# A decode kernel's page stage: probability transposes, the next unit's rotary scores and the products with keys in one piece

## The chip, the cores and the metric

The kernel runs on one core of one Trainium2 chip. The time is device time in microseconds for one execution. TensorE (PE) runs matmuls and transposes in the order of its program, and so do VectorE (DVE), ScalarE (ACT) and GpSimd (POOL); SyncE (SP) issues most transfers, POOL the indirect ones. An engine waits for another through semaphores only. Every instruction's place in its engine's queue is fixed when the program is built.

## The reference: what is computed

One layer of a decoder with two mixers, retention and latent attention (MLA), for a prompt of 1,024 tokens and for 8 sequences that decode 4 tokens each. All inputs and results are float32. The change lies wholly in the latent attention of the 8 decoding sequences over their past, 8,192 tokens each, which lie in pages of 128 tokens. For a sequence with query rows of 8 heads x 4 tokens, a past token has a latent row `ckv` of 256 numbers and a rotary row `kr` of 64:

```
score = (q_latent . ckv + q_rotary . kr) * scale
out   = softmax(score over past and new tokens) . ckv
```

The queries are turned into the latent space beforehand, so that the latent row is key and value in one. New tokens are masked causally; past tokens are all seen.

## The kernel before

The kernel is a row of stages. In the page stage, some 550 us long, two streams of work are woven together. One is `page_attention`, the decoding sequences' attention. The other is `fill`, a generator of gate projections for the prompt: for each block of weights (`wh`, `wl`, the upper and lower part of a weight block, made by ACT L247 and DVE L199 from `wr`), each product of a 128x128 block with 352 columns takes three matmuls, L266, L267 and L268, into the bank `mm`; after eight blocks ACT writes the sum out (`gev`, L413). `fill` depends on nothing in the page stage, so it is what PE does while the attention waits for other engines.

`beside` weaves: `page_attention` is a Python generator that yields a number wherever projections may stand, and for each unit of that number `fill` gets its share, 321 of 505 in all, at 0.441 a step of three matmuls (a yield of 12.0 is some 52 matmuls). What stands between two yields is a piece. Then the framework's scheduler puts the instructions of each engine in an order of its own that mostly keeps this one, but can move an instruction past others that it does not depend on, and so lets projections into a piece or takes DVE's work ahead of its place.

Sequences are taken in four groups `g` of two, and a group's past in four parts `jj` of 16 pages a sequence: 16 units. Ahead of a group's first unit stands `new_tokens(g)`, which scores the new tokens (L607, L608), exponentiates them (`pn`: DVE L612 and L613, ACT L614), transposes the result on PE (L617, copied by DVE L619) and multiplies with the new latents (L622). A unit in `past_keys` is:

- Gather: POOL fetches rotary rows into `rr` and latent rows into `craw` by indirect transfers (L588, L589). `rr` has two buffers, `craw` four: a unit uses two of each.
- Scores, five steps (L642): first the rotary rows (j=8), then four times 64 of the latent's 256 numbers. In each, DVE transposes 32x32 blocks into one of two ring buffers `kt` (L648, four instructions), and PE multiplies with the queries `q4` (L652, 16 matmuls on 32x32 tiles) into `sc`, of which there is one. `q4` holds the queries of two groups; those of the other two are stored to `q4D` (L578) from the tile `sel`, which takes one of the two `kt` ring buffers, and are read back at g=2 (L715).
- Softmax: ACT copies half of `sc` (L663), DVE adds the other half and takes the minimum (L664), ACT exponentiates to `pr` (L668) and makes the correction of the earlier sums (L670).
- A yield of 12.0, then eight transposes of `pr` on PE in two fours (L677), each copied to `pT` by DVE or ACT (L678), with a yield of 1.0 behind each four.
- Products with the keys: 32 matmuls (L683), added to `acc` by DVE (L685), and a yield of 1.0.

`ended` closes a group (L690 on).

Of the kernel before, what the change touches and what calls it, by code (L numbers as in the profile page):

```python
# [9 lines left out]
F32 = mybir.dt.float32  # L10
# [151 lines left out]
def decode_step(ctx: ExitStack, tc: tile.TileContext, A: dict, O: dict):  # L162
# [316 lines left out]
    def big(name, shape, rows_=P):  # L479
        return p3.tile([rows_, *shape], F32, tag="craw", name=name, bufs=4)  # L480
# [4 lines left out]
    def ring(name):  # L485
        return p3.tile([P, 4, 512], F32, tag="kt", name=name, bufs=2)
# [94 lines left out]
    rows_c = A["cache_ckv"].rearrange("l n (s a) c -> (l n s) (a c)", a=NA)  # L581
    rows_r = A["cache_krope"].rearrange("l n (s a) c -> (l n s) (a c)", a=NA)

    def gather(b, jj, c, r):

        at_ = b * (NPG // NA) + jj
        off = bass.IndirectOffsetOnAxis(ap=idx[:, at_:at_ + 1], axis=0)
        pool.indirect_dma_start(out=r, out_offset=None, in_=rows_r, in_offset=off)  # L588
        pool.indirect_dma_start(out=c, out_offset=None, in_=rows_c, in_offset=off)  # L589

    def new_tokens(g):

# [31 lines left out]
        yield 1.0  # L624
        return st

    def past_keys(g, jj, st):

        rr = [p3.tile([P, NA * ROPE], F32, tag="rr", name="rraw", bufs=2) for _ in range(2)]
        cr = [big("craw", (NA * KL,)) for _ in range(2)]
        for s in range(2):
            gather(2 * g + s, jj, cr[s], rr[s])
        keys = [c.rearrange("p (a d) -> p a d", a=NA) for c in cr]
        rope = [r.rearrange("p (a d) -> p a d", a=NA) for r in rr]
        yield 5.0  # L640
        sc = psg.tile([P, 4, 512], F32, tag="sc", name="sc", bufs=1)
        steps = [8, *range(0, 8, 2)]  # L642
        for n, j in enumerate(steps):
            kt = ring("kt")
            for i in range(2):
                for s in range(2):
                    src = keys[s][:, :, 32 * (j + i):32 * (j + i) + 32] if j < 8 else rope[s][:, :, 32 * i:32 * i + 32]
                    dve.transpose(kt[:, 2 * i + s].rearrange("p (n r) -> p n r", r=32), src)  # L648
            for q in range(4):
                qs_ = slice(32 * q, 32 * q + 32)  # L650
                for v in range(4):
                    pe.matmul(sc[32 * v:32 * v + 32, q, :], Q["q4"][qs_, j + v // 2, 2 * (g % 2) + v % 2, :], kt[qs_, v, :], start=n == 0,  # L652
                              stop=n == NJ // 2 - 1, tile_position=(32 * q, 32 * v), skip_group_check=True)
            if n + 1 < len(steps):
                yield 2.5
        sums = mid("sums", (4, 8, 32))
        acc, l, nm = st["acc"], st["l"], st["nm"]
        nm2 = p3.tile([P, 1], F32, tag="nm", name="nm", bufs=4)
        for half in range(2):
            hs = slice(64 * half, 64 * half + 64)  # L660
            even, odd = (sc[o:o + 64, :, 256 * half:256 * half + 256] for o in (0, 64))
            out = sums[hs].rearrange("p q n x -> p q (n x)")
            act.copy(out, odd)  # L663
            dve.tensor_tensor_reduce(out=out, in0=even, in1=out, scale=-1.0, scalar=nm[hs], op0=ALU.add, op1=ALU.min, accum_out=nm2[hs])  # L664
        st["nm"] = nm2
        pr = mid("pr", (8, 4, 32))
        lb = p3.tile([P, 1], F32, tag="lb", name="lb", bufs=2)
        act.activation(pr.rearrange("p n q x -> p q n x"), sums, AF.Exp, scale=-1.0, bias=nm2, accum_out=lb)  # L668
        corr = p3.tile([P, 1], F32, tag="corr", name="corr", bufs=2)
        act.activation(corr, nm, AF.Exp, scale=-1.0, bias=nm2)  # L670
        dve.scalar_tensor_tensor(out=l, in0=l, scalar=corr, in1=lb, op0=ALU.mult, op1=ALU.add)
        yield 12.0
        pT = mid("pT", (8, P))
        for u in range(2):
            pt = xb()
            for a in range(4):
                pe.transpose(pt[:, a * P:(a + 1) * P], pr[:, 4 * u + a].rearrange("p q x -> p (q x)"), ident)  # L677
            (act.copy if u % 2 else dve.tensor_copy)(pT[:, 4 * u:4 * u + 4, :], pt.rearrange("p (a r) -> p a r", a=4))  # L678
            yield 1.0
        pv = xb()  # L680
        for n in range(8):
            for v in range(4):
                pe.matmul(pv[32 * v:32 * v + 32, :KL], pT[:, n, 32 * v:32 * v + 32], keys[v % 2][:, 8 * (v // 2) + n, :], start=n == 0,  # L683
                          stop=n == 7, tile_position=(0, 32 * v), skip_group_check=True)
        dve.scalar_tensor_tensor(out=acc, in0=acc, scalar=corr, in1=pv[:, :KL], op0=ALU.mult, op1=ALU.add)  # L685
        yield 1.0

    def ended(g, st):

# [19 lines left out]
        return acc  # L709

    def page_attention():
        for g in range(4):
            if g == 2:
                q4 = q4_tile()
                sp.dma_start(q4, q4D)  # L715
                Q["q4"] = q4
            st = yield from new_tokens(g)
            for jj in range(NPG // NA):
                yield from past_keys(g, jj, st)
            last = ended(g, st)  # L720
        spare = ring("out")
        outs = [spare[:, g, :KL] for g in range(3)]
        for g in range(3):
# [879 lines left out]
```

## Time and profile before

| | |
|---|---|
| median of three runs | 2174.16 us (2173.42 to 2175.05) |
| the profiled execution | 2180.01 us, span 2178.2 us |
| mean granted clock of PE | 0.998 |
| busy: PE / its weight loads | 2135.6 us (98%) / 1856.0 us (85%) |
| busy: DVE / ACT / POOL | 1237.5 us (57%) / 729.6 us (33%) / 324.5 us (15%) |
| projections L266, L267, L268 (`xh`, `xl`), 1344 each | 457.1, 435.4 and 434.4 us busy |
| score steps L652, 2560 records | 91.4 us busy |
| transposes into `kt`, L648 on DVE, 256 | 160.7 us busy |

A profile row gives start, duration, engine, line, operation, output <- inputs, and behind it in brackets the idle time ahead of it and what ended it. Rows of the same kind that follow each other are joined (x4), and a float32 matmul of the attention leaves two records, so that 16 score matmuls read as x32. PE's matmuls are pipelined: the distance between two starts says more than a duration.

### The profile page before, as it was taken

The page shows a single profiled execution, that of the slowest core. Times are in us where ns is not written, and L with a number is a line of the kernel's source. Part 1 is how long each engine was busy: PE and PEld are TensorE (multiplying, and loading weights), DVE is VectorE, ACT ScalarE, POOL GpSimd, SP SyncE. Part 2 cuts the span into 40 slices and gives each one's busy share as a digit, 9 for nine tenths or more (in the row PEclk, how much of TensorE's full clock was granted, in tenths as well). Part 3 has the DMA queues.
Part 4 walks back from the last instruction along what each step waited for, and adds up shares of the span by engine and source line. Part 5 has one row for each costly group of instructions (what it writes and reads, how often), then busy time and mean ns, then how long its engine had stood idle before and what let it go on. Part 6 is the DMA issues. An engine that isn't in the chain of part 4 may idle for free.

```text
span 2178.2 us, 38580 instructions
## 1 busy us (share of the span) xinstructions
PE 2135.6 (98%) x15368; PEld 1856.0 (85%) x15368; DVE 1237.5 (57%) x2788; ACT 729.6 (33%) x1537; POOL 324.5 (15%) x519
## 2 busy tenths in 40 slices
PE   8999999999999999999999999899999999999998
PEld 7998777777777898888788887788888999999998
DVE  5414564555645356657666664778677353444465
ACT  6412232333333232221222311454556342222243
POOL 2211111111110022222121220122121000000022
PEclk9999999999999999999999999999999999999999
DMA  8447566565665421533614517110111453234243
GB/s 238 139 134 270 203 229 220 188 248 206 222 219 185 124 67 49 172 116 88 205 45 122 181 49 247 61 36 12 38 51 56 148 198 98 80 98 124 78 140 118
DMA packets 264357, 299.72 MB, mean 138 GB/s; under 512 B 26544, under 2 KB 221744, under 8 KB 260080
## 3 DMA queue, kind: packets, MB, share of 16 engines
q1 hardware_dynamic: 254960, 213.36, 31.6%
q0 software_dynamic: 9216, 83.89, 10.3%
q8 instruction: 121, 1.98, 0.4%
q14 instruction: 60, 0.49, 0.1%
HBM read 233.03 MB, written 64.17 MB: 136 GB/s over the span
## 4 chain that ended last, share of the span: by engine, by line
PE 62%; DVE 3%; issue 3%; DMA 1%; ACT 1%; POOL 1%; SPq 0%; ACTq 0%; POOLq 0%; DVEq 0%
PE mm L266 15%; PE mm L267 15%; PE mm L268 15%; PE ac L266 2%; PE ac L268 2%; PE ac L267 2%; PE mm L1302 2%; PE tr L1288 1%; PE sc L652 1%; PE tr L852 1%; PE ac L1245 1%; PE x L683 1%; PE ac L874 1%; PE ac L1246 1%; PE ac L1247 1%
## 5 line engine op out<-in xcount | busy, mean ns | idle before, releaser
L266 PE MATMUL mm<-xh,wh 128*128 128x352 f32 x1344 | 457.1, 340 | 0.9 <-ACT gev L413 0.7
L267 PE MATMUL mm<-xl,wh 128*128 128x352 f32 x1344 | 435.4, 324 | 0.0
L268 PE MATMUL mm<-xh,wl 128*128 128x352 f32 x1344 | 434.4, 324 | 0.0
L266 PEld LDWEIGHTS mm<-xh,wh 128*128 128x128 f32 x1344 | 252.2, 188 | 104.1 <-issue 86.5
L267 PEld LDWEIGHTS mm<-xl,wh 128*128 128x128 f32 x1344 | 253.3, 188 | 4.9 <-issue 2.7
L268 PEld LDWEIGHTS mm<-xh,wl 128*128 128x128 f32 x1344 | 253.1, 188 | 1.5 <-issue 1.5
L199 DVE TENSOR_TENSOR wl<-wr,wh 128x512 fp32r<-128x512 f32 (+2 forms) x251 | 172.2, 698 | 129.7 <-ACT wh L247 103.6
L247 ACT CAST wh<-wr 128x512 fp32r<-128x512 f32 x216 | 129.7, 618 | 277.6 <-PE mm L267 225.1
L648 DVE STREAM_TRANSPOSE kt<-craw 128x512 f32<-128x512 f32 x256 | 160.7, 681 | 106.8 <-PE sc L652 74.9
L413 ACT ACTIVATE gev<-mm 128x352 f32<-128x352 f32 x120 | 55.5, 463 | 229.4 <-PE mm L268 150.7
L268 PE MATMUL mm<-gh,wl 128*128 128x352 f32 x384 | 124.3, 324 | 0.0
L268 PE MATMUL mm<-mh,wl 128*128 128x352 f32 x384 | 124.3, 324 | 0.0
L266 PE MATMUL mm<-mh,wh 128*128 128x352 f32 x384 | 124.3, 324 | 0.0
L266 PE MATMUL mm<-gh,wh 128*128 128x352 f32 x384 | 124.2, 324 | 0.0
L267 PE MATMUL mm<-ml,wh 128*128 128x352 f32 x384 | 124.2, 324 | 0.0
L267 PE MATMUL mm<-gl,wh 128*128 128x352 f32 x384 | 124.2, 323 | 0.0
L266 PE MATMUL mm<-wv,xh 128*128 128x512 f32 x256 | 103.0, 402 | 0.0
L267 PE MATMUL mm<-wv,xh 128*128 128x512 f32 x256 | 100.9, 394 | 0.0
L268 PE MATMUL mm<-wv,xl 128*128 128x512 f32 x256 | 100.7, 393 | 0.0
L841 ACT ACTIVATE on<-ac,gb,gs 128x512 f32<-128x512 f32 (+1 forms) x36 | 28.0, 777 | 208.4 <-DVE gb L839 208.2
L652 PE MATMUL sc<-kt,q 32*32 32x512 f32 x2560 | 91.4, 600 | 0.0
L1533 POOL TENSOR_TENSOR xr<-x1h,x1l 128x352 f32<-128x352 f32 x24 | 26.9, 1145 | 389.9 <-DVE pT L199 311.6
(388 smaller groups left out, 4569.6 us busy)
## 6 DMA issues: line engine op xcount, KB each, us to landing
wr<-in_w_in_dram SPq DMA_DIRECT2D x144, 256.0 KB, 3.0
st<-in_state_ret_dram SPq DMA_DIRECT2D x32, 512.0 KB, 4.0
out_ret_sample_dram<-st SPq DMA_DIRECT2D x32, 512.0 KB, 3.6
wr<-in_w_ple_gate_dram SPq DMA_DIRECT2D x48, 256.0 KB, 2.8
gt<-gev SPq DMA_DIRECT2D x48, 176.0 KB, 1.8
gl<-go SPq DMA_DIRECT2D x16, 528.0 KB, 7.5
gate<-ga SPq DMA_DIRECT2D x16, 528.0 KB, 3.3
g<-gt SPq DMA_DIRECT2D x32, 256.0 KB, 3.1
```

The lines of the kernel that those rows point to most:

```text
L199: dve.tensor_tensor(out=out, in0=src, in1=b32(hi), op=ALU.subtract)
L247: hi_by[0](hi, raw)
L266: pe.matmul(out, wh, xh, start=first, stop=False)
L267: pe.matmul(out, wh, xl, start=False, stop=False)
L268: pe.matmul(out, wl, xh, start=False, stop=last)
L413: act.activation(t, ps, func)
L648: dve.transpose(kt[:, 2 * i + s].rearrange("p (n r) -> p n r", r=32), src)
L652: pe.matmul(sc[32 * v:32 * v + 32, q, :], Q["q4"][qs_, j + v // 2, 2 * (g % 2) + v % 2, :], kt[qs_, v, :], start=n == 0, stop=n == NJ // 2 ...
L683: pe.matmul(pv[32 * v:32 * v + 32, :KL], pT[:, n, 32 * v:32 * v + 32], keys[v % 2][:, 8 * (v // 2) + n, :], start=n == 0, stop=n == 7, til ...
L841: act.activation(on[:n], po, AF.Identity, bias=nb[:n], scale=s[:n])
L1302: pe.matmul(po[:, :256], v[a][w], t[:, x, 256 * a:256 * a + 256], start=j + a + part == 0, stop=False, skip_group_check=True)
L1533: pool.tensor_tensor(out=xr, in0=b32(x1[f][0][:, sl]), in1=b32(x1[f][1][:, sl]), op=ALU.add)
```

## The change

A unit becomes an object `Unit` whose gathers are issued when it is made, and it is made at the start of the unit ahead: the rotary rows of both sequences first, then the latent rows. Its rotary step is taken out of its own scores: DVE's four transposes stand behind the softmax of the unit ahead, and PE's 16 score matmuls between that unit's transposes of probabilities and its products with keys. The three together have no yield between them; the yields that stood there and behind the products (1.0 three times) and one score yield (2.5) go into the yield ahead of the piece, 12.0 to 17.5. The first unit has no unit ahead, so its gather and its rotary step stand at the start of the stage, ahead of `new_tokens(0)`. The reload of `q4` moves into the last unit of g=1, behind its last score. A unit's yields still add up to 30; the first unit's gather adds a yield of 5.0 to the whole.

```diff
--- before.py
+++ after.py
@@ -581,12 +581,11 @@
     rows_c = A["cache_ckv"].rearrange("l n (s a) c -> (l n s) (a c)", a=NA)
     rows_r = A["cache_krope"].rearrange("l n (s a) c -> (l n s) (a c)", a=NA)
 
-    def gather(b, jj, c, r):
+    def gather(b, jj, src, out):
 
         at_ = b * (NPG // NA) + jj
         off = bass.IndirectOffsetOnAxis(ap=idx[:, at_:at_ + 1], axis=0)
-        pool.indirect_dma_start(out=r, out_offset=None, in_=rows_r, in_offset=off)
-        pool.indirect_dma_start(out=c, out_offset=None, in_=rows_c, in_offset=off)
+        pool.indirect_dma_start(out=out, out_offset=None, in_=src, in_offset=off)
 
     def new_tokens(g):
 
@@ -624,35 +623,55 @@
         yield 1.0
         return st
 
-    def past_keys(g, jj, st):
-
-        rr = [p3.tile([P, NA * ROPE], F32, tag="rr", name="rraw", bufs=2) for _ in range(2)]
-        cr = [big("craw", (NA * KL,)) for _ in range(2)]
-        for s in range(2):
-            gather(2 * g + s, jj, cr[s], rr[s])
-        keys = [c.rearrange("p (a d) -> p a d", a=NA) for c in cr]
-        rope = [r.rearrange("p (a d) -> p a d", a=NA) for r in rr]
-        yield 5.0
-        sc = psg.tile([P, 4, 512], F32, tag="sc", name="sc", bufs=1)
-        steps = [8, *range(0, 8, 2)]
-        for n, j in enumerate(steps):
+    class Unit:
+
+        def __init__(self, g, jj):
+            self.g = g
+            rr = [p3.tile([P, NA * ROPE], F32, tag="rr", name="rraw", bufs=2) for _ in range(2)]
+            cr = [big("craw", (NA * KL,)) for _ in range(2)]
+            for rows_, to in ((rows_r, rr), (rows_c, cr)):
+                for s in range(2):
+                    gather(2 * g + s, jj, rows_, to[s])
+            self.keys = [c.rearrange("p (a d) -> p a d", a=NA) for c in cr]
+            self.rope = [r.rearrange("p (a d) -> p a d", a=NA) for r in rr]
+            self.sc = None
+
+        def turn(self, j):
             kt = ring("kt")
             for i in range(2):
                 for s in range(2):
-                    src = keys[s][:, :, 32 * (j + i):32 * (j + i) + 32] if j < 8 else rope[s][:, :, 32 * i:32 * i + 32]
+                    src = (self.keys[s][:, :, 32 * (j + i):32 * (j + i) + 32] if j < 8 else
+                           self.rope[s][:, :, 32 * i:32 * i + 32])
                     dve.transpose(kt[:, 2 * i + s].rearrange("p (n r) -> p n r", r=32), src)
+            return kt
+
+        def score(self, j, kt, first=False, last=False):
+            if first:
+                self.sc = psg.tile([P, 4, 512], F32, tag="sc", name="sc", bufs=1)
             for q in range(4):
                 qs_ = slice(32 * q, 32 * q + 32)
                 for v in range(4):
-                    pe.matmul(sc[32 * v:32 * v + 32, q, :], Q["q4"][qs_, j + v // 2, 2 * (g % 2) + v % 2, :], kt[qs_, v, :], start=n == 0,
-                              stop=n == NJ // 2 - 1, tile_position=(32 * q, 32 * v), skip_group_check=True)
-            if n + 1 < len(steps):
+                    pe.matmul(self.sc[32 * v:32 * v + 32, q, :], Q["q4"][qs_, j + v // 2, 2 * (self.g % 2) + v % 2, :], kt[qs_, v, :],
+                              start=first, stop=last, tile_position=(32 * q, 32 * v), skip_group_check=True)
+
+    def past_keys(unit, st, ahead):
+
+        nxt = Unit(*ahead) if ahead else None
+        yield 5.0
+        for j in range(0, 8, 2):
+            unit.score(j, unit.turn(j), last=j == 6)
+            if j < 6:
                 yield 2.5
+        sc, keys = unit.sc, unit.keys
+        if nxt and nxt.g == 2 and unit.g == 1:
+            q4 = q4_tile()
+            sp.dma_start(q4, q4D)
+            Q["q4"] = q4
         sums = mid("sums", (4, 8, 32))
         acc, l, nm = st["acc"], st["l"], st["nm"]
         nm2 = p3.tile([P, 1], F32, tag="nm", name="nm", bufs=4)
@@ -669,21 +688,24 @@
         corr = p3.tile([P, 1], F32, tag="corr", name="corr", bufs=2)
         act.activation(corr, nm, AF.Exp, scale=-1.0, bias=nm2)
         dve.scalar_tensor_tensor(out=l, in0=l, scalar=corr, in1=lb, op0=ALU.mult, op1=ALU.add)
-        yield 12.0
+        if nxt:
+            kt = nxt.turn(8)
+        yield 17.5
         pT = mid("pT", (8, P))
         for u in range(2):
             pt = xb()
             for a in range(4):
                 pe.transpose(pt[:, a * P:(a + 1) * P], pr[:, 4 * u + a].rearrange("p q x -> p (q x)"), ident)
             (act.copy if u % 2 else dve.tensor_copy)(pT[:, 4 * u:4 * u + 4, :], pt.rearrange("p (a r) -> p a r", a=4))
-            yield 1.0
+        if nxt:
+            nxt.score(8, kt, first=True)
         pv = xb()
         for n in range(8):
             for v in range(4):
                 pe.matmul(pv[32 * v:32 * v + 32, :KL], pT[:, n, 32 * v:32 * v + 32], keys[v % 2][:, 8 * (v // 2) + n, :], start=n == 0,
                           stop=n == 7, tile_position=(0, 32 * v), skip_group_check=True)
         dve.scalar_tensor_tensor(out=acc, in0=acc, scalar=corr, in1=pv[:, :KL], op0=ALU.mult, op1=ALU.add)
-        yield 1.0
+        return nxt
 
     def ended(g, st):
 
@@ -709,15 +731,16 @@
         return acc
 
     def page_attention():
-        for g in range(4):
-            if g == 2:
-                q4 = q4_tile()
-                sp.dma_start(q4, q4D)
-                Q["q4"] = q4
-            st = yield from new_tokens(g)
-            for jj in range(NPG // NA):
-                yield from past_keys(g, jj, st)
-            last = ended(g, st)
+        places = [(g, jj) for g in range(4) for jj in range(NPG // NA)]
+        unit = Unit(0, 0)
+        yield 5.0
+        unit.score(8, unit.turn(8), first=True)
+        for n, (g, jj) in enumerate(places):
+            if jj == 0:
+                st = yield from new_tokens(g)
+            unit = yield from past_keys(unit, st, places[n + 1] if n + 1 < len(places) else None)
+            if jj + 1 == NPG // NA:
+                last = ended(g, st)
         spare = ring("out")
         outs = [spare[:, g, :KL] for g in range(3)]
         for g in range(3):
```

Line numbers after the change: gathers L588, new tokens L606, L607, L611, L612, L613, L616, L618, L621, transposes into `kt` L645, scores L654, minimum L683, exponent L687, transposes of `pr` L698, their copies L699, products L705.

First PE's queue around the transposes of one unit, before; `x<-cst,pr` are the transposes, `x<-craw,pT` the products.

```order
L677 MATMUL x<-cst,pr 128x128 x4
L266 MATMUL mm<-xh_113,wh 128x352
L267 MATMUL mm<-xl_114,wh 128x352
L268 MATMUL mm<-xh_113,wl 128x352
L266 MATMUL mm<-xh_115,wh 128x352
L267 MATMUL mm<-xl_116,wh 128x352
L268 MATMUL mm<-xh_115,wl 128x352
L677 MATMUL x<-cst,pr 128x128 x4
L266 MATMUL mm<-xh_117,wh 128x352
L267 MATMUL mm<-xl_118,wh 128x352
L268 MATMUL mm<-xh_117,wl 128x352
L683 MATMUL x<-craw,pT 32x256 x32
```

Nine projections part the three pieces. The same place on PE after:

```order
L268 MATMUL mm<-xh_119,wl 128x352
L698 MATMUL x<-cst,pr 128x128 x8
L654 MATMUL sc<-kt,q_2158 32x512 x16
L705 MATMUL x<-craw,pT 32x256 x32
L266 MATMUL mm<-xh_121,wh 128x352
```

The eight transposes, the next unit's rotary scores and the products follow each other. It reads so in eleven of the sixteen units; in units 8, 10, 11 and 13 (counted from 0) 12 to 21 projections still stand inside the piece, and in the last unit, which has no next one, three.

Next PE's queue at the start of the stage, from the end of the queries (`tr<-qrT,sel`) on: the new tokens' scores (`x<-kvST,qlT`, `x<-krST,qrT`), before.

```order
L571 MATMUL tr<-qrT,sel 128x256 x2
L266 MATMUL mm<-xh_115,wh 128x352
L267 MATMUL mm<-xl_116,wh 128x352
L268 MATMUL mm<-xh_115,wl 128x352
L266 MATMUL mm<-xh_117,wh 128x352
L267 MATMUL mm<-xl_118,wh 128x352
L268 MATMUL mm<-xh_117,wl 128x352
L266 MATMUL mm<-xh_119,wh 128x352
L607 MATMUL x<-kvST,qlT 64x32 x2
L608 MATMUL x<-krST,qrT 64x32
```

Seven projections stand ahead of them. PE after, from the last projection ahead of the same three matmuls on:

```order
L268 MATMUL mm<-xh_113,wl 128x352
L654 MATMUL sc<-kt,q_2158 32x512 x16
L606 MATMUL x<-kvST,qlT 64x32 x2
L607 MATMUL x<-krST,qrT 64x32
L266 MATMUL mm<-xh_115,wh 128x352
L267 MATMUL mm<-xl_116,wh 128x352
```

Now 24 projections instead of seven stand between `tr<-qrT,sel` and this piece, which begins with the first unit's rotary scores; twelve projections follow it, then the transpose of `pn` (L616), six more and L621.

Last DVE's queue at the same place: `q_2158` are the queries, `pn` and `nm` the new tokens' scores and their maximum, `pnT` the copied transpose; before.

```order
L573 COPY q_2158<-tr 128x256 x5
L612 TENSOR_TENSOR pn<-x,cst 64x32
L613 TENSOR_REDUCE nm<-pn 64x1
L619 COPY pnT<-x 32x64
L648 STREAM_TRANSPOSE kt<-craw 128x512 x4
L199 TENSOR_TENSOR wl<-wr,wh 128x512 x2
L648 STREAM_TRANSPOSE kt<-craw 128x512 x12
```

The new tokens' three instructions come ahead of all transposes of latents. DVE after, from the same copies on:

```order
L573 COPY q_2158<-tr 128x256 x5
L645 STREAM_TRANSPOSE kt<-craw 128x512 x4
L199 TENSOR_TENSOR wl<-wr,wh 128x512 x2
L645 STREAM_TRANSPOSE kt<-craw 128x512
L611 TENSOR_TENSOR pn<-x,cst 64x32
L645 STREAM_TRANSPOSE kt<-craw 128x512
L612 TENSOR_REDUCE nm<-pn 64x1
L645 STREAM_TRANSPOSE kt<-craw 128x512 x2
L618 COPY pnT<-x 32x64
```

The same three instructions now stand behind the first unit's first latent transposes and between the next ones.

## The prediction

> **What bounds the kernel now.** I read the page's busy table first, then the busy time of the page stage (about 197 to 745 us, the only stretch that the change touches), then the timeline of each engine around one piece of a unit and around the start of the stage, and last who waits for the softmax lines.
>
> ```profile
> PE 2135.6 (98%) x15368; PEld 1856.0 (85%) x15368; DVE 1237.5 (57%) x2788; ACT 729.6 (33%) x1537; POOL 324.5 (15%) x519
> 197.00:745.00 548.00, 543.25 (x5964) 419.86 (x5963) 306.90 (x551) 179.42 (x295) 54.16 (x63) 1.00 0.57 202
> L677 PE MATMUL x<-cst,pr x128: 270/272/330, 227.8 to 734.4; 128*128 128x128 f32 x128
>   ACT pr L668: 6.8, 15
> L683 PE MATMUL x<-craw,pT x1024: 379/379/403, 230.2 to 738.8; 128*32 128x256 f32 x171
>   DVE pT L678: 4.7, 6
> ```
>
> The second row is the page stage (columns: length, then busy time of PE, PE's weight loads, DVE, ACT and POOL, granted clock, DMA share, GB/s): of 548 us PE is busy 543.25 (DVE 306.90, ACT 179.42), at clock 1.00. PE is the bound there, so a change is worth what it takes from PE's own stream: switches between kinds of matmul, and the few us in which PE waits. The last rows say where PE waits: before the transposes of the probabilities (L677) for the exponent, 6.8 us on 15 occasions, and before the products (L683) for the copied transposes, 4.7 us on 6. These counts overlap with the pipeline; from start to start less is lost, as worked out below.
>
> **Fewer switches.** A unit's score step, its two fours of transposes and its products each stand alone between projections:
>
> ```profile
> 301.90 0.32 PE L268 MATMUL mm<-xh,wl 128*128 128x352 f32 x1
> 302.15 1.14 PE L652 MATMUL sc<-kt,q 32*32 32x512 f32 x32
> 303.22 0.43 PE L266 MATMUL mm<-xh,wh 128*128 128x352 f32 x1
> 303.49 0.32 PE L267 MATMUL mm<-xl,wh 128*128 128x352 f32 x1
> ...
> 229.06 0.32 PE L268 MATMUL mm<-xh,wl 128*128 128x352 f32 x1
> 229.22 0.60 PE L677 MATMUL x<-cst,pr 128*128 128x128 f32 x4
> 229.82 0.33 PE L267 MATMUL mm<-xl,wh 128*128 128x352 f32 x1
> 229.99 0.32 PE L268 MATMUL mm<-xh,wl 128*128 128x352 f32 x1
> 230.23 3.66 PE L683 MATMUL x<-craw,pT 128*32 128x256 f32 x64
> 233.82 0.43 PE L266 MATMUL mm<-xh,wh 128*128 128x352 f32 x1
> 234.09 0.32 PE L267 MATMUL mm<-xl,wh 128*128 128x352 f32 x1
> ...
> 34.08 1.04 PE L322 MATMUL tr<-cst,xt 128*128 128x128 f32 x8
> 34.87 0.42 PE L266 MATMUL ac<-wlh,xh 128*32 128x384 f32 x1
> ```
>
> Projections start 0.1625 us apart. Taking those pitches out: from 301.90 to 303.49 a score step costs 1.59 - 2 x 0.1625 = 1.27; four transposes, 229.06 to 229.82, 0.44; the products, 229.99 to 234.09, 3.78. Together, with two fours, 5.93. In one piece stand eight transposes in a row (0.79, from 34.08 to 34.87), the score (1.07 from start to next start), the products (3.59) and the way out (0.27 - 0.16 = 0.11): 5.56 if a change of kind inside the piece costs nothing, 5.74 if the 0.09 by which a start after a projection is late (0.25 against 0.16) is paid twice. So 0.18 to 0.36 a unit, 0.27 taken, and 15 units have a successor: 4.1 (2.7 to 5.4). The built order does not keep all pieces whole: in four of the sixteen units 12 to 21 projections still stand inside, each at about 0.15 more, 0.6 back. At the group borders the new tokens' matmuls now stand directly behind the products (at the start, behind the first rotary score), four joins at about 0.15: 0.6 gained. Switches: **-4.1** (-2.5 to -5.5).
>
> **Waits that go.** The largest wait of each kind:
>
> ```profile
> 564.11 0.33 PE L268 MATMUL mm<-xh,wl 128*128 128x352 f32 x1
> 565.16 0.65 PE L677 MATMUL x<-cst,pr 128*128 128x128 f32 x4 [0.72 <-ACT pr L668]
> ...
> 326.45 0.32 PE L268 MATMUL mm<-xh,wl 128*128 128x352 f32 x1
> 328.04 3.66 PE L683 MATMUL x<-craw,pT 128*32 128x256 f32 x64 [1.27 <-DVE pT L678]
> ```
>
> Against an undisturbed 0.16, the transposes at 565.16 start 0.89 late; summed like that over the 16 units, with 0.05 more inside eleven of them, they lose 4.3. The products at 328.04 start 1.34 late against 0.25; with one more case (0.62) they lose 2.0. Together 6.3. In after, 75 projections instead of 51 to 54 stand ahead of the transposes in 11 units: some 21 x 0.1625 = 3.4 us more for the exponent, four times the largest lateness, so those waits go. In the four split units and the last one it is 54 to 63, 0 to 1.5 us more, so some stays. Before the products, the next unit's score now covers the copies: DVE's copy can begin 0.68 after the first transpose (227.76 to 228.44 in the row below) and takes 0.69, so it is done at 1.4, while the products are due at 0.79 + 1.07 = 1.9. ACT copies the second four meanwhile; that half is needed only in the second half of the products. I leave 1.1 of the 6.3 standing: **-5.2** (-3.5 to -6.3).
>
> ```profile
> 227.76 0.65 PE L677 MATMUL x<-cst,pr 128*128 128x128 f32 x4
> 228.44 0.69 DVE L678 COPY pT<-x 128x512 f32<-128x512 f32 x1 [0.31 <-PE x L677]
> ```
>
> **A new wait at the start of the stage.** Before, the first group's new tokens come ahead of everything of the first unit:
>
> ```profile
> 197.96 0.42 PE L607 MATMUL x<-kvST,qlT 128*64 128x32 f32 x4
> 198.53 0.43 PE L267 MATMUL mm<-xl,wh 128*128 128x352 f32 x1
> 199.87 0.23 PE L617 MATMUL x<-cst,pn 64*32 64x64 f32 x1
> ...
> 198.71 0.18 DVE L612 TENSOR_TENSOR pn<-x,cst 64x32 f32<-64x32 f32 x1 [1.55 <-PE x L608]
> 198.93 0.18 DVE L613 TENSOR_REDUCE nm<-pn 64x1 f32<-64x32 f32 x1
> 205.09 2.49 DVE L648 STREAM_TRANSPOSE kt<-craw 128x512 f32<-128x512 f32 x4 [4.74 <-DMA q4D<-sel]
> 207.50 1.25 DVE L199 TENSOR_TENSOR wl<-wr,wh 128x512 fp32r<-128x512 f32 x2
> 208.67 4.86 DVE L648 STREAM_TRANSPOSE kt<-craw 128x512 f32<-128x512 f32 x8
> ...
> 199.14 0.32 ACT L614 ACTIVATE pn<-pn,nm 64x32 f32<-64x32 f32 x1 [1.57 <-DVE nm L613]
> ```
>
> The transposes at 205.09 sit in a ring buffer that the stores of `sel` to q4D must first leave; they have landed when DVE starts at 205.09, and the change moves neither. In after, DVE's queue holds those four transposes, two subtractions `wl`, and one transpose ahead of `pn`, and one more ahead of `nm`. So: 205.09, transposes to 207.50, `wl` to 208.67, a transpose (2.41 / 4 = 0.60) to 209.27, `pn` to 209.49 (0.22 from start to start), a transpose to 210.09, `nm` to 210.30, the exponent, and the transpose of `pn` on PE 0.73 after the exponent's start (199.14 to 199.87): 211.0. PE gets there earlier: 17 projections more than before ahead of the first piece put it at 197.96 + 2.76 = 200.7, the rotary score (whose own transposes DVE did long before) 1.07, the three new-token matmuls 0.57, twelve projections 2.15: 204.5. PE is in order, so it waits **6.5 us** (5.5 to 7.5). Queued behind are only projections, which could have run. Nothing later in the stage gives it back, as PE is the bound throughout. At the three other group borders the stores are long gone, and the chain is as short as before (9 to 26 projections stand between): nothing added.
>
> **The clock after that wait.** PE never stands still that long inside this trace, but at its ends it does:
>
> ```profile
> 4.85 1.94 PE L322 MATMUL tr<-cst,xt 128*128 128x128 f32 x8 [4.85 <-DMA cst<-in_consts_dram]
> 11.30 0.49 PE L268 MATMUL ac<-wlh,xl 128*128 128x384 f32 x1
> ...
> 2168.62 0.97 PE L1507 MATMUL tr<-cst,yT 128*128 128x128 f32 x3 [0.76 <-DVE yT L1538]
> ...
> 2171.00:2172.00 1.00, 0.00 (x0) 0.00 (x0) 0.86 (x3) 0.66 (x3) 0.95 (x2) 1.00 0.00 0
> 2172.00:2173.00 1.00, 0.00 (x0) 0.00 (x0) 0.50 (x1) 0.65 (x2) 0.00 (x0) 0.53 0.78 311
> ```
>
> After the last matmuls (2169.6) the granted clock falls to half at about 2172; a 6.5 us wait is over twice that. At the start eight transposes take 1.94 instead of 1.04, and matmuls stay slow until about 11.5: 2.4 us of dense work (from 9.1) to 6.7 us in all. Half rate for that long loses 1.2 to 3.4; I take 2.3, times 0.85 for the case that the wait is cut up or misses it: **+2.0** (0 to 3.4). The Trainium skill (TensorE: Matmul & The Clock Gate, Part 1: The HAM clock gate) states the rule: one idle window of about 3.4 us halves the clock, about 3.4 us of work restores it. The trace's 2.4 us of idleness at its end is of that kind, if shorter. By the page the loss would be an estimated 1.7, and the sum 0.3 lower.
>
> **The rest.** The gathers stay where buffers come free (the products' release of `craw`, the transposes' release of the rope rows), on POOL, which is 15% busy; rope rows ahead of latents costs nothing while that holds, and a late gather would show as DVE waiting for it. The reload of q4 on SP is issued behind the last score of the group ahead; its first user, the rotary score in the next piece, now stands 75 projections (12 us) behind that:
>
> ```profile
> DMA to landing us min/median/max: 5.7/6.5/7.4
> ```
>
> The slowest transfer of q4D takes 7.4, so PE does not wait for it. The built order loads ACT's tables 36 times instead of 32 in the stage; ACT is a third busy, but a projection's evacuation stands behind it: +0.5 (0 to 1.5).
>
> **Sum**: 6.5 + 2.0 + 0.5 - 5.2 - 4.1 = -0.3 us on the profiled execution's 2180.01 us, so 2179.7 there. The median of the runs is 2174.16, 5.85 lower; a difference in PE's stream carries over: 2173.9 us.
>
> **Rivals.**
> *Faster*: the wait at the start does not happen or is short, because the stores of `sel` land earlier. For it: only one transfer sets it, in a stretch where the DMA is loaded with latents. Against: nothing ahead of 196 us is changed. Without wait and clock loss the sum is -0.3 - 8.5 = -8.8: 2165.4. The upper end of both savings with the wait gives -11.8 + 9.0 = -2.8, 2171.4: not enough alone.
> *Slower*: the products wait for `pT`, with no projections left between. In about half of the units the built order has the pair `wl` directly ahead of DVE's copy (as at 328.04, where it cost 1.34). If the pair ends over 0.5 us after the transposes are done, the products start late; a pair begun at the worst time, 1.17, leaves 1.17 - 0.5 = 0.67. In eight units 5.4: sum +5.1, 2179.3. Against: the pair is due once in 72 projections, so it seldom meets that moment.
> *The change does less than it says*: the built order splits more pieces in effect, as the four; each split costs 0.15, so this moves the time by under 1 us.
>
> **Chances.** Below 0.2% (4.35 us), about what a measurement of this kernel can tell from no change, I call it the same. The likeliest, savings and the wait nearly cancelling, 0.56 (own range 2169.8 to 2178.4); faster by the first rival, or by a cheap clock with savings that I have not seen, 0.22; slower by the second, or by a longer wait with a cold clock and small savings, 0.22. To leave out no more than two in ten the range goes from 2166.5 (most of the first rival's case is outside) to 2180.0 (past the second's).
>
> **What would show it.** In the profile after: a wait of 5.5 to 7.5 before the new tokens' transpose near 205, released by the exponent, with slow matmuls and a granted clock near 0.5 behind it; no wait for the exponent but in split units; a piece of 5.6 to 5.7 from first transpose to the next projection's second start; no new wait before the products. Wrong would be: no such wait (then faster), or waits for `pT` in many units (then slower).

## The result, and the profile after

The changed kernel takes 2181.02 us (median of six runs, 2179.28 to 2183.44), the kernel before, in the same set, 2173.76 us (2171.34 to 2175.05). The ratio is 1.0033, 95% interval 1.0023 to 1.0043: 7.3 us slower. The profiled execution of the changed kernel took 2179.5 us (span 2177.7), that of before 2180.01, so by the two traces alone the change would have gained half a microsecond. That contradiction is what the experiments had to settle.

The page's busy row of the changed kernel, and two stretches of its timeline by windows (length, busy time of PE, its loads, DVE, ACT and POOL, granted clock, DMA share, GB/s):

```profile
PE 2133.4 (98%) x15368; PEld 1865.0 (86%) x15368; DVE 1239.9 (57%) x2788; ACT 734.9 (34%) x1541; POOL 325.7 (15%) x519
203.00:210.00 7.00, 1.09 (x7) 0.81 (x5) 5.17 (x11) 0.10 (x1) 0.00 (x0) 0.73 0.15 38
211.00:217.00 6.00, 6.00 (x21) 4.86 (x21) 0.18 (x2) 0.83 (x2) 0.00 (x0) 0.55 0.09 32
```

PE does next to nothing from 204 to 210 us, and behind that its granted clock is near half (0.55). The timelines of PE and of DVE at that place show why:

```profile
203.77 0.32 PE L268 MATMUL mm<-xh,wl 128*128 128x352 f32 x1
210.37 0.28 PE L616 MATMUL x<-cst,pn 64*32 64x64 f32 x1 [6.27 <-ACT pn L613]
210.58 0.66 PE L266 MATMUL mm<-xh,wh 128*128 128x352 f32 x1
211.04 0.49 PE L267 MATMUL mm<-xl,wh 128*128 128x352 f32 x1
...
216.47 0.33 PE L266 MATMUL mm<-xh,wh 128*128 128x352 f32 x1
...
204.83 2.49 DVE L645 STREAM_TRANSPOSE kt<-craw 128x512 f32<-128x512 f32 x4 [8.12 <-DMA q4D<-sel]
207.24 1.25 DVE L199 TENSOR_TENSOR wl<-wr,wh 128x512 fp32r<-128x512 f32 x2
208.41 0.70 DVE L645 STREAM_TRANSPOSE kt<-craw 128x512 f32<-128x512 f32 x1
209.04 0.14 DVE L611 TENSOR_TENSOR pn<-x,cst 64x32 f32<-64x32 f32 x1
```

The wait is the predicted one, 6.3 us, with the predicted chain: the stores of `sel` land, four transposes, `wl`, one more, and only then `pn`. From 210.58 to 216.47 PE runs 15 projections and L621 in 5.89 us; at full clock these take 15 x 0.1622 + 0.77 = 3.20, so the half clock costs another 2.7.

A merged piece of the changed kernel, in PE's timeline:

```profile
241.92 1.03 PE L698 MATMUL x<-cst,pr 128*128 128x128 f32 x8
242.89 1.14 PE L654 MATMUL sc<-kt,q 32*32 32x512 f32 x32
243.96 3.68 PE L705 MATMUL x<-craw,pT 128*32 128x256 f32 x64
247.56 0.43 PE L266 MATMUL mm<-xh,wh 128*128 128x352 f32 x1
247.83 0.32 PE L267 MATMUL mm<-xl,wh 128*128 128x352 f32 x1
```

From 241.92 to 247.83, less the pitch of one projection: 5.75. That is the upper end of the predicted 5.56 to 5.74: the transposes take 0.97 until the scores start instead of 0.79, the rest is as predicted. In the rest of the page stage this trace regains everything: counted by projections done, it is 7.0 us behind the first trace of before at 294 us of the latter, and 2.1 ahead at 732. Behind the stage 1.6 of that is lost again; the last projections end 0.5 apart.

### The profile page after: what moved, and what is told of

Same layout as the page of the kernel before. It is cut to its first block, busy times and chain, and to the rows that moved or that the text cites. A ratio compares the mean times of both kernels' runs of the same rounds, so it can differ in the third digit from the quotient of the medians.

```text
span 2177.7 us, 38592 instructions
## 1 busy us (share of the span) xinstructions
PE 2133.4 (98%) x15368; PEld 1865.0 (86%) x15368; DVE 1239.9 (57%) x2788; ACT 734.9 (34%) x1541; POOL 325.7 (15%) x519
## 4 chain that ended last, share of the span: by engine, by line
PE 87%; issue 5%; DVE 3%; DMA 2%; POOL 1%; ACT 1%; SPq 0%; POOLq 0%; DVEq 0%; ACTq 0%
PE mm L266 21%; PE mm L268 20%; PE mm L267 20%; PE sc L654 4%; PE x L705 3%; PE ac L267 2%; PE ac L266 2%; PE ac L268 2%; PE mm L1325 2%; PE tr L1311 1%; PE ac L1268 1%; PE tr L875 1%; PE ac L897 1%; PE ac L1269 1%; PE x L698 1%
## 5 line engine op out<-in xcount | busy, mean ns | idle before, releaser
L645 DVE STREAM_TRANSPOSE kt<-craw 128x512 f32<-128x512 f32 x256 | 162.4, 684 | 94.2 <-PE sc L654 80.4
L654 PE MATMUL sc<-kt,q 32*32 32x512 f32 x2560 | 92.3, 600 | 0.0
```

Of the source, the lines that this page charges most:

```text
L654: pe.matmul(self.sc[32 * v:32 * v + 32, q, :], Q["q4"][qs_, j + v // 2, 2 * (self.g % 2) + v % 2, :], kt[qs_, v, :], start=first, stop=las ...
```

## The experiments

All ratios are to the kernel before, run in turns with it on the same chip. The sets ran on three chips, and on each the kernel before takes 2180.6 to 2183.4 us, 7 to 10 more than in the first measurement.

### Both kernels again

No edit.

> The kernel before, unchanged, for a second trace. Its first profiled execution took 2180.01 us and its median 2173.8, so something in that execution was some 6 us slower than usual. Theory one: the 6 us lay in the page stage, so that the usual stage is shorter than the trace showed and the change had less to save (page stage here about 6 us shorter than in the first trace). Rival: they lay behind the stage, in the stretch from 745 to 1500 us, where PE waits for DMA now and then (page stage here as in the first trace, within 1 us, the rest 6 us shorter). Ratio to before 1.000 either way.

> The changed kernel, unchanged, for a second trace beside the second one of before. Both theories: about 2181 us, 1.0033 times before, with the wait of about 6.3 us for the new tokens' exponent near 204 us and about 10 us of half clock behind it. If the wait is not there in this trace, it depends on when a transfer lands and not on the order alone.

Measured: before 2180.82 against 2180.66, ratio 0.9998 (0.9989 to 1.0007); the changed kernel 2185.23, ratio 1.0021 (1.0010 to 1.0032), 4.6 us slower. In the new trace of before the page stage is as in the first trace to 1.1 us, and the whole span is 1.7 longer. Neither theory holds as it was put: the first trace of before is not slow for this chip, and it is the runs at 2174 us that differ from it. The wait at the start is there again, 8.2 us this time, and by the working of the section above the half clock behind it costs 3.3:

```profile
211.58 0.29 PE L616 MATMUL x<-cst,pn 64*32 64x64 f32 x1 [8.21 <-ACT pn L613]
```

But the rest of the stage regains less than in the first trace of the changed kernel. The same score step, the last of a unit, in that first trace and in this one (PE, ACT and POOL):

```profile
493.65 1.14 PE L654 MATMUL sc<-kt,q 32*32 32x512 f32 x32
494.80 0.94 POOL L588 DMA_INDIRECT rraw<-in_cache_krope_dram,idx  x1 [8.48 <-DVE kt L645]
496.05 0.94 POOL L588 DMA_INDIRECT rraw<-in_cache_krope_dram,idx  x1 [0.30 <-DVE kt L645]
495.14 1.01 ACT L682 COPY sums<-sc 64x1024 f32<-64x1024 f32 x1 [3.26 <-PE sc L654]
```

```profile
496.08 1.14 PE L654 MATMUL sc<-kt,q 32*32 32x512 f32 x32
497.22 0.95 POOL L588 DMA_INDIRECT rraw<-in_cache_krope_dram,idx  x1 [7.39 <-DVE kt L645]
498.47 0.94 POOL L588 DMA_INDIRECT rraw<-in_cache_krope_dram,idx  x1 [0.30 <-issue]
500.00 1.01 ACT L682 COPY sums<-sc 64x1024 f32<-64x1024 f32 x1 [5.70 <-PE mm L268]
...
506.49 1.28 ACT L413 ACT_TABLE_LOAD   x1
507.79 0.46 ACT L413 ACTIVATE gev<-mm 128x352 f32<-128x352 f32 x1
...
508.31 0.43 PE L266 MATMUL mm<-xh,wh 128*128 128x352 f32 x1 [1.07 <-ACT gev L413]
```

The scores are as long in both. In the first trace ACT is released 1.5 us after their start, in the second 3.9, and with ACT so much later a projection's evacuation queues behind the softmax and a table load, and PE waits 1.07 for it. Measured over all units, the end of the last score step is signalled 3 us or more after its start in 14 of 16 units of the second trace of the changed kernel, in 12 and 13 of the two traces of before, and in the first trace of the changed kernel never (1.3 to 1.5 us there). Each late signal overlaps POOL's two gathers of rotary rows and comes mostly 0.5 to 0.7 us behind the second one's end. It is PE's signal that is late, and not ACT: where ACT has to wait, its copy starts within 0.1 us of the change of PE's semaphore, in the traces with late signals and without.

### The new tokens first, and the rotary scores first

The changed kernel with the old order at the start (tokens_first):

```diff
         unit = Unit(0, 0)
+        st = yield from new_tokens(0)
         yield 5.0
         unit.score(8, unit.turn(8), first=True)
         for n, (g, jj) in enumerate(places):
-            if jj == 0:
+            if n and jj == 0:
                 st = yield from new_tokens(g)
```

> The changed kernel, but the first group's new tokens stand ahead of the first unit's rotary scores again, so that DVE has their maximum before the transposes that wait for the stores of sel. The wait and the half clock behind it are the loss (theory): about 9 us less than the changed kernel, 2172 us; if moreover the 10.8 us that the trace gained in the rest of the stage are gained in every run, 2163. Rival, that the loss lies in the merged pieces or behind the stage: 2179 to 2182.

Measured: 2176.39, ratio 0.9977 (0.9966 to 0.9987), which is 8.8 us under the changed kernel in the same set. The wait and the half clock, 9.0 us together in the first trace and 11.5 in the second, account for the whole loss within the intervals (some 3 us either way on this difference), and without them the change gains 4.3 here. The transpose of `pn` now stands at 200.91 us without a wait.

The converse, before with this one part of the change (score_first):

```diff
-            if n + 1 < len(steps):
+            if st is None:
+                st = yield from new_tokens(g)
+            elif n + 1 < len(steps):
                 yield 2.5
...
-            st = yield from new_tokens(g)
+            st = (yield from new_tokens(g)) if g else None
             for jj in range(NPG // NA):
-                yield from past_keys(g, jj, st)
+                st = yield from past_keys(g, jj, st)
```

> The kernel before with this one part of the change alone: in the first unit the rotary scores stand ahead of the new tokens. Theory (wait and half clock): a wait of 6 to 7 us for the new tokens' exponent and 2 to 3 us of slow matmuls, 9 us over before, 2183 us. Rival, that the old kernel's looser order absorbs the wait: within 2 us of before.

Measured: 2192.15, ratio 1.0052 (1.0039 to 1.0064), 11.5 us over before. The wait in its trace:

```profile
212.83 0.28 PE L617 MATMUL x<-cst,pn 64*32 64x64 f32 x1 [5.99 <-ACT pn L614]
213.04 0.66 PE L266 MATMUL mm<-xh,wh 128*128 128x352 f32 x1
213.50 0.49 PE L267 MATMUL mm<-xl,wh 128*128 128x352 f32 x1
```

The theory holds; the rival, that a looser order absorbs it, falls. The 2.5 us beyond the expected 9 are not accounted for: the trace has more waits for the exponent (5.8 us of idle time ahead of ten transposes, 2.1 ahead of seven in the second trace of before), but counted by projections its stage as a whole loses 9.6, and about 1 us of the distance stands ahead of the stage.

### Distance and merging apart

The changed kernel with the new tokens first and the merged piece at the old distance (old_spacing), and at a distance between (merged_66; 15.5 and 2.0 instead of 12.0 and 5.5). The diff leaves out the lines of tokens_first, which both have too:

```diff
-        yield 17.5
+        yield 12.0
...
+        yield 5.5
         return nxt
```

> The changed kernel with the new tokens first, but the merged piece stands where the transposes stood before: a yield of 12.0 ahead of it and 5.5 behind it, 51 to 54 projections ahead instead of 75. It has the fewer switches but not the longer distance. If the saving is mostly switches (4.1 predicted) and the piece's score covers the copies, it keeps 4 to 6 us: 0.9972 to 0.9985. If the distance is what saves, it has the waits for the exponent back (4.3) and is at 0.9985 to 1.000.

The pieces of before with more distance (before_spacing):

```diff
-        yield 5.0
+        yield 1.5
...
-        yield 12.0
+        yield 15.5
```

> The kernel before with its pieces as they are, but a yield of 15.5 instead of 12.0 ahead of the transposes and 1.5 instead of 5.0 at a unit's start: 66 to 69 projections instead of 51 to 54 ahead of the transposes. Distance without merging: the waits for the exponent (4.3 us) go, about 0.998. If the waits are not what costs the time, or come back as waits for ACT's evacuation or for the transposes at the unit's start, 0.9995 to 1.001.

> The changed kernel with the new tokens first and a yield of 15.5 ahead of the merged piece and 2.0 behind it: 66 projections ahead of it, as in before_spacing, so that the two differ by the merging alone. Both have no waits for the exponent to speak of. If merging saves what the traces' pieces show (5.75 for the merged one against 1.27 + 2 x 0.44 + 3.79 = 5.94 apart: 0.19 x 15 = 2.8 us, and 2 us of waits of the products), it is 3 to 5 us under before_spacing's 0.9985: 0.996 to 0.997. If the merged piece brings waits for ACT's evacuation (2.5 us more in the trace of tokens_first), it is 0.9975 to 0.9985.

Measured: old_spacing 1.0007 (0.9997 to 1.0016), before_spacing 0.9985 (0.9976 to 0.9994), merged_66 0.9968 (0.9958 to 0.9978). At the old distance merging gains nothing that can be measured: its pieces wait for the exponent, and once for DVE's copy, as the trace of old_spacing shows (what the transposes wait for, matmuls and weight loads counted together as in the 6.8 us on 15 occasions of before, and the one wait of the products):

```profile
L698 PE MATMUL x<-cst,pr x128: 270/273/329, 229.4 to 733.7; 128*128 128x128 f32 x128
  ACT pr L687: 10.1, 18
329.31 3.66 PE L705 MATMUL x<-craw,pT 128*32 128x256 f32 x64 [1.42 <-DVE pT L699]
```

The matmuls alone wait for the exponent 3.6 us on eight occasions there, 1.8 on five and 2.1 on seven in the first two traces of before. Distance alone gains 3.3 us. Merging at that distance gains another 3.7 by the ratios (0.9985 to 0.9968), but these two ran on different chips, their intervals overlap, and by their medians (2176.96 and 2175.36) they are 1.6 apart. So where the signals are late the gain of distance is shown, and that merging adds to it is likely, but not shown.

### Moving the gathers away

First attempt (before_late_gather): POOL copies the unit ahead's sums ahead of the gathers.

```diff
+        if LB[0] is not None:
+            held = p3.tile([P, 1], F32, tag="held", name="held", bufs=2)
+            pool.tensor_copy(held, LB[0])
         for s in range(2):
             gather(2 * g + s, jj, cr[s], rr[s])
```

> The kernel before, but POOL copies one column of the preceding unit's sums (lb) ahead of a unit's gathers, so that the two gathers of rotary rows are issued about 7 us later, behind the preceding unit's softmax, instead of just when its last score step ends. In both traces of before the end of a unit's last score step is signalled 3.1 to 3.5 us after its start, in other steps 1.5, and the late ones are those with the two gathers running. Theory (the gathers hold the signal back): all last steps signalled after 1.5 us, the waits for the exponent (4.3 us) gone, 3 to 4 us faster than before, ratio 0.998 to 0.9985. Rival (the last step of a unit signals late for a reason of its own): lags unchanged, ratio 1.000.

> The changed kernel with the new tokens first (as in tokens_first) and the same delay of the gathers. Theory: last steps signalled after 1.5 us, and the four waits for ACT's evacuation (3.6 us from start to start in the trace of tokens_first) gone too, since ACT's softmax starts 2 to 2.5 us earlier: 2 to 4 us less than tokens_first, ratio to before 0.996 to 0.997. Rival: same as tokens_first, 0.9977.

Measured: 1.0026 (1.0015 to 1.0038) and 1.0012 (1.0003 to 1.0021), both slower than without the edit (the second against the 0.9977 of tokens_first, on another chip), and the signals as late as ever. The edit missed: the copy was scheduled behind the gathers. What it did was to add a reader of `lb`, for which ACT has to wait. Eleven of the 16 exponents have a table load right ahead of them. In the first trace of before none of the eleven loads waits, and `nm` is mostly still being made while they run; in the trace of before_late_gather nine of them come only behind `nm`. One unit in each:

```profile
529.29 1.28 ACT L668 ACT_TABLE_LOAD   x1
530.58 1.15 ACT L668 ACTIVATE pr<-sums,nm 128x1024 f32<-128x1024 f32 x1
```

```profile
533.41 1.28 ACT L673 ACT_TABLE_LOAD   x1 [0.94 <-DVE nm L669]
534.71 1.15 ACT L673 ACTIVATE pr<-sums,nm 128x1024 f32<-128x1024 f32 x1
```

Second attempt: DVE reads a column of the rotary buffers together with the unit's correction, so that they come free only behind the softmax. In before (before_rr_held; there a unit's own rotary rows with the correction of the unit ahead), in the changed kernel with the new tokens first (tokens_first_rr_held), and in the changed kernel itself (after_rr_held):

```diff
         if nxt:
             kt = nxt.turn(8)
+            for r in nxt.rr:
+                held = p3.tile([P, 1], F32, tag="held", name="held", bufs=2)
+                dve.scalar_tensor_tensor(out=held, in0=r[:, :1], scalar=corr, in1=r[:, 1:2], op0=ALU.mult, op1=ALU.add)
```

> The kernel before, but DVE reads one column of the next unit's two rotary buffers together with the unit's correction, behind the softmax, so that these buffers come free, and POOL gathers into them, some 7 us after the last score step instead of at its end (the run before_late_gather did not move them: its extra copy stood behind the gathers, and its wait went ahead of the exponent's table load). Theory (the two gathers hold back PE's signal): last score steps signalled 1.5 us after their start in all units, softmax 2 us earlier, the waits for the exponent (4.3 us from start to start) gone, 3 to 4.5 us faster than before, 0.998 to 0.9985. Rival (the last step signals late for another reason): lags of 3 us or more stay, ratio 1.000 to 1.0005 (32 small DVE instructions beside PE).

> The changed kernel with the new tokens first and the same hold on the rotary buffers. Theory: last steps signalled after 1.5 us, and with ACT's softmax 2 us earlier the four waits for ACT's evacuation (3.3 us in the trace of tokens_first) are gone or halved: 0.996 to 0.997 of before. Rival (lags stay, or the waits for ACT have another cause): as tokens_first, 0.9977.

Measured, in one set: before_rr_held 2172.30, ratio 0.9955 (0.9942 to 0.9968); tokens_first_rr_held 2170.84, ratio 0.9947 (0.9933 to 0.9961). In both traces all last score steps are signalled within 1.5 us of their start. The first unit's last step in the second trace of before (PE, POOL, ACT), and in that of before_rr_held:

```profile
219.42 1.14 PE L652 MATMUL sc<-kt,q 32*32 32x512 f32 x32
219.71 0.94 POOL L588 DMA_INDIRECT rraw<-in_cache_krope_dram,idx  x1 [29.85 <-DVE kt L648]
220.95 0.94 POOL L588 DMA_INDIRECT rraw<-in_cache_krope_dram,idx  x1 [0.30 <-issue]
222.50 1.01 ACT L663 COPY sums<-sc 64x1024 f32<-64x1024 f32 x1 [8.39 <-PE mm L268]
```

```profile
217.29 1.14 PE L658 MATMUL sc<-kt,q 32*32 32x512 f32 x32
218.62 1.01 ACT L669 COPY sums<-sc 64x1024 f32<-64x1024 f32 x1 [6.64 <-PE sc L658]
225.74 0.93 POOL L588 DMA_INDIRECT rraw<-in_cache_krope_dram,idx  x1 [38.02 <-DVE held L649]
```

ACT is released 1.3 us after the step's start instead of 3.1, and no wait for the exponent, the copies or an evacuation is left in the stage in either kernel. On top of that the merging and its distance are worth 1.5 us in time, less than the intervals resolve. In the two traces the stage gains 4.1 of PE's time, as much as was predicted for the switches, and 2.5 of it is gone again by 1310 us, in the stages behind. PE's waits there for state loads and weight casts are 0.8 us longer (1.4 against 0.6), so most of that loss stays unexplained.

> The changed kernel as it is (rotary scores ahead of the new tokens, so with the wait at the start), with the hold on the rotary buffers. Theory: without late signals the change has only its switches to save (about 4 us in the stage) and the wait with its half clock to pay (about 9), so it is 5 to 9 us over before_rr_held in the same call, though well under after_again. Rival (the change's 4.6 us with late signals are all there is, whatever the signals): within 3 us of before_rr_held plus 4.6 by chance alone cannot be told; it falls if the difference is over 6 or under 3.

> The same kernel as before_rr_held, so that the pair with after_rr_held stands on one chip and against the same runs of before: 0.9955 again, 8 to 12 us under before, if this chip has the late signals; within 2 us of before on a chip that has none.

> The kernel before, for a third trace beside this pair: last score steps signalled 3 us or more after their start in most units, as in its first two traces; where the median of before is near 2174 instead of 2181, signalled after 1.5 us, as in the first trace of the changed kernel.

Measured: after_rr_held 2179.77, ratio 0.9989 (0.9980 to 0.9998); before_rr_held 2173.88, ratio 0.9961 (0.9949 to 0.9974); the third trace of before, 2180.45, has the late signals in 12 units. So with all signals in time the change costs 5.9 us, against 4.6 with late ones and 7.3 in the first measurement. The theory's 5 to 9 holds, but the rival, that the change costs the same whatever the signals, does not fall either: it was to fall over 6 or under 3, and the difference of 1.3 between the first two is not beyond their intervals. By time alone it is open whether late signals alter what the change costs.

The traces tell more. Take the wait and the half clock at the start as lost, and count by projections how far the two kernels are apart at the end of the stage; the rest is what the change saves in it. It saves some 10.5 us from the first trace of before to the first of the changed kernel, where before has late signals and the changed kernel none; 6.8 from before_again to after_again, where both have them; and 5.0 from before_rr_held to after_rr_held, where neither has. 9.3 was predicted.

## Why the prediction was wrong

It was 2173.9 us with a range to 2180.0; the result is 2181.02, slower, where the same time was forecast. For the profiled execution the working gave 2179.7, and the changed kernel's took 2179.5. That agreement is luck in part: the trace of before has late signals and that of the changed kernel has none, and the change is not what removes them, as its second trace shows.

- **A new wait at the start of the stage** was right: 6.5 us predicted, 6.3 measured in the first trace, 8.2 in the second, by the chain given, step by step. Taking it out alone (tokens_first) gives 8.8 us back with its half clock.
- **The clock after that wait** was right in kind and 0.7 too small: 2.0 predicted, 2.7 measured in the first trace, 3.3 in the second. The trace of before holds a nearer row than its two ends, which the working did not use: a stop of 2.95 us inside the kernel, and half the clock behind it.

```profile
1409.98 0.50 PE L1245 MATMUL ac<-k,q 128*128 128x512 f32 x1 [2.95 <-ACT pr L1263]
1411.00:1414.00 3.00, 3.00 (x11) 2.42 (x11) 1.46 (x4) 1.18 (x3) 1.02 (x1) 0.50 0.02 5
```

- **Fewer switches** was right for the stage: 4.1 predicted, 4.1 between the two traces without late signals (before_rr_held and tokens_first_rr_held), of which later stages take 2.5 back; in time 1.5 is left, within the noise. A piece saves 0.19, at the low end of 0.18 to 0.36.
- **Waits that go**, -5.2, is the step that failed. The waits in the trace of before are real, and in the changed kernel they are gone, as predicted, but their cause is that the end of a unit's last score step is signalled mostly 1.6 to 2.4 us late while POOL issues two gathers. Where signals are in time, before has no such waits (before_rr_held), and the change has nothing to save there. Where they are late, the longer distance removes them, but the late softmax then holds up ACT's evacuations.
- **The rest**, +0.5 for evacuations behind ACT's extra table loads, was too small where signals are late: four such waits, 3.3 us from start to start, in the trace of tokens_first and again in the second of the changed kernel, against one of 0.9 in before. In the first trace of the changed kernel there is none.
- **The sum's carrying over to the runs** failed with it. The profiled execution of before was 5.85 us above the median; the working took that as a shift common to both kernels. In the experiments, taking the late signals out brings before from 2183.4 and 2182.6 us to 2172.3 and 2173.9, the level of the first measurement; so they can make the whole of such a difference. That the runs at 2174 had no late signals is not shown, as none of them left a trace of before; it fits the trace of the changed kernel, which is of one of its timed runs and has none. If so, 9.0 (6.3 + 2.7) was lost in those runs, and the 7.3 measured leaves 1.7 gained: a remainder, not a measurement of its own, but close to the 1.5 that the change is worth by time in the set without late signals. So for the runs of the result the cause stays argued in this one point.
- **The rivals.** The faster one, stores that land early, did not happen. The slower one, products that wait for `pT`, hardly happened: nothing in the first trace of the changed kernel and 0.15 us in the second, 1.42 us once at the old distance and 0.68 once in merged_66; the score step between covers most of the copies. The splits were not as harmless as said where signals are late: three of the four waits for an evacuation in the second trace of the changed kernel stand right behind the first transposes of a split piece. What the splits cost by themselves was not measured.

The version faster than both kernels is the changed one with the new tokens first and the gathers held (tokens_first_rr_held), 0.9947 of before; before with the gathers held alone is at 0.9955 and 0.9961, not distinguishable from it in time.

## What to carry to other kernels

When a profiled execution is several microseconds off the median of the runs, find what differs before summing a change against it: waits of the profile may not exist in the runs, and a saving made of them is worth nothing there. A step taken out of a chain's order must be checked on every in-order queue for what it now stands behind; here one transfer's landing, through a shared ring buffer, stopped TensorE for 6 us and halved its clock for as long again.

## What the runs showed of the hardware that was not expected

- TensorE's signal of a finished step can come late: 3.0 to 3.9 us after the step's start instead of 1.3 to 1.5 in 12 to 14 of 16 units, always with two indirect gathers being issued by POOL, and in time once these are moved 7 us away. In the first trace of the changed kernel the same overlap delays nothing. Why one trace differs stays open, and so does what in the gathers holds the signal back.
- A wait that an exponent on ACT needs can stand at the table load ahead of it: with one more reader of a small tile, nine of the eleven table loads ahead of exponents came only behind `nm`, which puts up to their 1.3 us on the path. The run with it is 5.7 us slower by its ratio; that this wait is all of it is not shown.
- The stop of 6.3 us left the clock at half for some 6 us of work, in which a projection took 0.29 us from start to start instead of 0.16; the stop of 8.2 us in the second trace did so for some 7 us.
